# Two dense pairs of row tiles instead of three, K renumbered, and w loaded one k-slice at a time, in a Strassen-Winograd QKV projection

## The chip, the cores and the metric

The kernel runs on one core of a Trainium2 chip. The metric is device time in microseconds (us) of one execution; lower is better. Engine names are those of the profile: PE (TensorE matmul), PEld (its weight load), DVE (VectorE), ACT (ScalarE), POOL (GpSimd), SP (SyncE, which here only issues DMAs).

## The reference

One float32 matrix product, cut into three outputs:

```python
x     : (16, 512, 768) float32        # 8192 rows of K = 768
w_qkv : (768, 2304)    float32
qkv = np.matmul(x, w_qkv)
q, k, v = qkv[..., :768], qkv[..., 768:1536], qkv[..., 1536:]
return np.stack([q, k, v], axis=0).astype(np.float32)
```

x is 25.2 MB, w 7.08 MB and the output 75.5 MB.

## The kernel before, in words

**Tiling.** The 8192 rows are 32 *pairs* of 128-row tiles. The 2304 columns are two *quads* q = 0 and 1 of 1024 columns each, and a rest of 256 columns between them. K = 768 is split into KT = 6 slices of 128, which lie on the partitions; KH = 3 slices are one half. A pair and a quad together form a 2x2 by 2x2 block product (two row tiles, two halves of K, two blocks of 512 columns).

**Two ways to do a pair.** For the first NS = 3 pairs `block` does a dense product: for each quad and each of its two 512-column blocks, two row tiles times six matmuls, so 48 matmuls of 128x512 in bf16 for a pair. For pairs 3 to 31 `two` (and `last`) uses Strassen-Winograd: seven products of three matmuls per quad, so 42 for a pair. In `do(u, n)` products 1 and 2 use plain bf16 copies of x and w; products 3 to 7 use sums of blocks in f32r: of x (`s`, made by POOL in `sums_x`) and of w (`t`, made by DVE in `sum_w`; `b22` is a plain copy). Products 1, 6, 7 and 4 accumulate one after another in the same PSUM bank `u.x`, and ACT copies the bank out between them; 5 and 3 share `u.y`. I call them P1 to P7. `rem` does the 256 rest columns of a pair with 12 matmuls of 128x256.

**x.** A pair done densely is loaded by rows (`load_rows`), cast to bf16 by DVE and ACT (`cast_rows`), turned by 12 PE transposes and copied out of PSUM (`turn_rows`). A pair done with sums is loaded by `load_x` in four DMAs of 32 partitions, turned by one DVE 32x32 block transpose (`transpose`, L130), rounded to bf16 by POOL (`round_x`, L175) and summed by POOL (`sums_x`, L183 to L187).

**K numbering.** K is numbered `(p j)`: partition p holds rows 6p to 6p+5 of w. So the transposes read every sixth element, and one partition's six slices are six neighbouring rows of w.

**w.** `load_w` (L89) takes rows `"(p j) n -> p j n"` and issues one DMA for as many slices as it is given. The first block of quad 0 is loaded in six DMAs of one slice, the other three blocks in two DMAs of three slices each, and the 256 rest columns (`st_rem`) in one DMA. The blocks land in fp32 staging tiles; DVE and ACT cast them (`cast`, `cast_k`), and `sum_w` subtracts them.

**Order.** The schedule is written out by hand (`manual_schedule`): every engine runs its instructions in program order. All loads of the start are on SP's queue, in the order x0, x1, w(0,0), `st_rem`, x2, w(0,1), w(1,0), w(1,1), x3. Here w(q,c) is block c of quad q. A DMA reports on one of eight semaphores, taken in turn, and SP issues it only after the DMA eight places before it has landed. The PE order is: warm-up matmuls on zeros (`busy`, L365), transposes and the dense block (0,0) of pairs 0 and 1, their rests, pair 2's transposes and block (0,0), then blocks (0,1), (1,0), (1,1) of all three pairs, pair 2's rest, and then `two` for pair 3 onward. Stores are on SP's queue after those loads. The output tiles `o` come from a pool of five and those of the rest columns (`orem`) from a pool of two, so a tile is written again only after its store has landed.

Of the kernel before, what the change touches and what calls it, by code (L numbers as in the profile page):

```python
# [10 lines left out]
def kernel(  # L11
# [20 lines left out]
    nc = tc.nc  # L32
    P = 128
# [51 lines left out]


    def load_w(dst, j0, nj, off, cols):
        rows = w_qkv.rearrange("(p j) n -> p j n", j=KT)
        nc.sync.dma_start(dst, rows[:, j0:j0 + nj, off:off + cols])  # L89

    stage = {}

    def load_blocks(q, c, nj=KH):
        if q == 0:
            t = tq_pool.tile([P, KT, CB], fp32, name="st0", tag="tq")
            for j in range(0, KT, nj):
                load_w(t[:, j:j + nj], j, nj, Q_OFF[q] + c * CB, CB)
            stage[q, 0, c], stage[q, 1, c] = t[:, :KH, :], t[:, KH:, :]
        else:
            for h in range(2):  # L100
                t = st_pool.tile([P, KH, CB], fp32, name="st1", tag="st")
                load_w(t[:], h * KH, KH, Q_OFF[q] + c * CB, CB)
                stage[q, h, c] = t[:]

    def sum_w(q, n):
        t1, t2, t3, t4 = ts[q]
        o, in0, in1 = {
            1: (t1, stage[q, 0, 1], stage[q, 0, 0]),
            2: (t2, stage[q, 1, 1], t1),
            3: (t3, stage[q, 1, 1], stage[q, 0, 1]),  # L110
            4: (t4, stage[q, 1, 0], t2),
        }[n]
        nc.vector.tensor_tensor(o, in0, in1, op=sub)
# [5 lines left out]
    def load_x(p, other):  # L119
        xin[p] = xin_pool.tile([P, 2 * P // G, KC], fp32, name="xin")  # L120
        t = xin[p]
        rows = x_flat[p * 2 * P:(p + 1) * 2 * P, :].rearrange("(g b) k -> b g k", b=G)
        for n in range(2):
            for h in range(2):
                i = 2 * h + n
                (nc.sync, other)[h].dma_start(t[i * G:(i + 1) * G], rows[:, :, i * KC:(i + 1) * KC])

    def transpose(p):
        t = xf_pool.tile([P, KT, 2 * P], fp32, name="xf")
        nc.vector.transpose(  # L130
            t[:].rearrange("p j (g b) -> p g j b", b=G),
            xin.pop(p)[:].rearrange("p g (a j) -> p g j a", a=G),
        )
        xf[p] = t

# [2 lines left out]
    def load_rows(p):  # L138
        xin[p] = xin_pool.tile([P, 2, K], fp32, name="xin")
        rows = x_flat[p * 2 * P:(p + 1) * 2 * P, :]  # L140
        nc.sync.dma_start(xin[p][:], rows.rearrange("(r m) k -> m r k", m=P))

    def copy_halves(dst, src, two):

        nc.vector.tensor_copy(out=dst[0], in_=src[0])  # L145
        if two:
            nc.scalar.activation(dst[1], src[1], ident)  # L147
        else:
            nc.vector.tensor_copy(out=dst[1], in_=src[1])
# [3 lines left out]
    def cast_rows(p, two=True):  # L153
        src = xin.pop(p)
        xc[p] = s_pool.tile([P, 2, K], bf16, name="xc", tag="s")
        for r in range(2):
            halves = (slice(0, K // 2), slice(K // 2, K))
            copy_halves([xc[p][:, r, n] for n in halves], [src[:, r, n] for n in halves], two)

    def turn_rows(p, two=True):  # L160
        c = xc.pop(p)
        xb[p] = xb_pool.tile([P, KT, 2 * P], bf16, name="xb", tag="xb")
        for r in range(2):
            cols = c[:, r, :].rearrange("m (p j) -> m j p", j=KT)
            ps = ps_pool.tile([P, KT, P], bf16, name="ps")
            for j in range(KT):
                nc.tensor.transpose(ps[:, j, :], cols[:, j, :], eye)  # L167
            ks = (slice(0, KH), slice(KH, KT))
            copy_halves(
                [xb[p][:, n, r * P:(r + 1) * P] for n in ks], [ps[:, n, :] for n in ks], two  # L170
            )

    def round_x(p):
        xb[p] = xb_pool.tile([P, KT, 2 * P], bf16, name="xb", tag="xb")
        nc.gpsimd.tensor_copy(out=xb[p][:], in_=xf[p][:])  # L175
# [18 lines left out]
    def quad(p, q):  # L194
        u = Quad()
        u.p, u.q = p, q
        u.o = o_pool.tile([P, 2, 2 * CB], fp32, name="o", tag="o")
        u.x = u.y = u.z = None
        return u
# [67 lines left out]
    def rem(p):  # L267
        ps = ps_pool.tile([P, 2, REM], fp32, name="ps")
        for r in range(2):
            rem_row(p, r, ps[:, r, :])  # L270
        o = or_pool.tile([P, 2, REM], fp32, name="orem")
        nc.scalar.activation(o[:], ps[:], ident)  # L272
        nc.sync.dma_start(rows_of(1, p, R_OFF - H, R_OFF - H + REM), o[:])
# [67 lines left out]
        rem_stored(1)  # L341


    NS = 3
    zero = xb_pool.tile([P, CB], bf16, name="zero", tag="xb")
    nc.vector.memset(zero[:], 0.0)  # L346
    load_rows(0)
    nc.scalar.activation(tiny[:], zero[:, :1], ident)
    make_identity(nc, eye)
    load_rows(1)  # L350
    load_blocks(0, 0, 1)
    st_rem = o_pool.tile([P, KT, REM], fp32, name="str", tag="o")
    load_w(st_rem[:], 0, KT, R_OFF, REM)
    load_rows(2)
    load_blocks(0, 1)
    load_blocks(1, 0)
    load_blocks(1, 1)
    load_x(3, nc.sync)
    quads = [[quad(p, q) for p in range(NS)] for q in range(2)]

    def busy(n):

        ps = bank()
        for _ in range(n):
            nc.tensor.matmul(ps[:], zero[:, :P], zero[:], start=True, stop=True)  # L365

    def cast(q, h, c, w, eng):

        dst = w[:, h * KH:(h + 1) * KH, :]
        if eng is nc.scalar:  # L370
            eng.activation(dst, stage[q, h, c], ident)
        else:
            eng.tensor_copy(out=dst, in_=stage[q, h, c])

    def block(q, c, w, groups, cast_next):


        ps = {}
        for js, tiles in groups:
            for n in tiles:  # L380
                p, r = divmod(n, 2)
                if n not in ps:
                    ps[n] = bank()
                for j in js:
                    nc.tensor.matmul(  # L385
                        ps[n][:], xb[p][:, j, r * P:(r + 1) * P], w[:, j, :],
                        start=(j == 0), stop=(j == KT - 1), skip_group_check=True,
                    )
                if KT - 1 not in js:
                    continue  # L390
                if r == 0:
                    cast_next(p)
                u = quads[q][p]
                nc.scalar.activation(u.o[:, r, c * CB:(c + 1) * CB], ps[n][:], ident)
                if c == 1 and r == 1:
                    store_quad(u)

    def halves(tiles):
        return [(range(h * KH, (h + 1) * KH), tiles) for h in range(2)]


    singles = [((0, ), (0, 1)), ((1, ), (0, 1)), ((0, 1), (2, 3))]
    singles += [((j, ), range(4)) for j in range(2, KT)]

    act, dve = nc.scalar, nc.vector
    def cast_k(j):
        dve.tensor_copy(out=b1[0][:, j, :], in_=stage[0, j // KH, 0][:, j % KH, :])

    def cast_next(q, c, w):
        return lambda p: p < 2 and cast(q, p, c, w, act)  # L410

    def cast_k(j):
        dve.tensor_copy(out=b1[0][:, j, :], in_=stage[0, j // KH, 0][:, j % KH, :])

    nothing = lambda p: None
    busy(11)
    cast_rows(0)
    turn_rows(0)
# [7 lines left out]
    act.activation(w_rem[1][:], st_rem[:, KH:], ident)  # L426
    dve.tensor_copy(out=w_rem[0][:], in_=st_rem[:, :KH])
    bt0 = bt_pool.tile([P, KT, CB], bf16, name="bt")
    bt1 = bt_pool.tile([P, KT, CB], bf16, name="bt")

    block(0, 0, b1[0], singles, nothing)
    rem(0)
    rem(1)
    cast_rows(2, False)
    turn_rows(2, False)
    block(0, 0, b1[0], halves((4, 5)), nothing)
    for h in range(2):
        cast(0, h, 1, bt0, dve)
    for n in range(1, 5):
        sum_w(0, n)  # L440
    dve.tensor_copy(out=b22[0][:], in_=stage[0, 1, 1])
    block(0, 1, bt0, halves(range(6)), cast_next(1, 0, b1[1]))
    load_x(4, nc.sync)
    block(1, 0, b1[1], halves(range(6)), cast_next(1, 1, bt1))
    block(1, 1, bt1, halves(range(6)), nothing)
    rem(2)
    t_1 = [tq_pool.tile([P, 2, KH, CB], f32r, name=f"t_1{n}", tag="tq") for n in range(2)]
    ts[1] = [t_1[n // 2][:, n % 2] for n in range(4)]
    sum_w(1, 1)
    sum_w(1, 2)  # L450
    transpose(3)
    round_x(3)
    sums_x(3)
    sum_w(1, 3)
    sum_w(1, 4)
    dve.tensor_copy(out=b22[1][:], in_=stage[1, 1, 1])

    for p in range(NS, NP):
        def early():
            if p + 1 < NP:  # L460
                transpose(p + 1)
                round_x(p + 1)
                sums_x(p + 1)
            if p + 2 < NP:
                load_x(p + 2, nc.scalar)

        if p < NP - 1:
            two(quad(p, 0), quad(p, 1), early)
        else:
            last(quad(p, 0), quad(p, 1))  # L470
# [30 lines left out]
```

## Time and profile before

| what | value |
|---|---|
| median of 3 runs (lowest to highest) | 362.73 us (362.67 to 363.09) |
| span of the profiled execution | 361.3 us |
| the profiled execution's own time | not listed apart from its span; the median lies 1.4 us above the span |
| PE busy | 353.4 us (98%), 1765 instructions |
| DVE, ACT, POOL busy | 224.4, 182.9, 173.9 us |
| DMA | 108.08 MB, mean 299 GB/s |
| one pair of `two`, start to start | 10.74 us |
| start of pair 3 (first matmul of `two`) | 45.43 us |

How to read it: an engine's busy time is summed over the span, so it is an average over the start, the 29 like pairs and the end. The chain that ended last follows work back from the last instruction. Times within the span are us from its start. "GB/s" and "DMA share" are what the core's 16 DMA engines moved and the mean share of time in which they had packets under way; packets overlap a little, so a full share reads slightly above 1.

### The profile page before, as it was taken

The numbers are of one execution on the slowest core, as the hardware profiler recorded it, in microseconds if no ns is written. First come the engines' busy times: TensorE is split into PE (matmuls) and PEld (weight loads), VectorE is DVE, ScalarE is ACT, GpSimd is POOL, SyncE is SP. The second block draws the span as 40 slices with busy tenths as digits, with TensorE's granted clock in tenths as the row PEclk, the third lists the DMA queues.
The fourth block names the chain that finished last, engine by engine and source line by source line (L and its number), as shares of the span: only waits on it lengthen the run. The fifth ranks groups of instructions, "written<-read, shape, count | busy, mean of one in ns | idle before, by whom it ended". The sixth has DMA issues, their size and how long they took to land.

```text
span 361.3 us, 5221 instructions
## 1 busy us (share of the span) xinstructions
PE 353.4 (98%) x1765; PEld 251.0 (69%) x1797; DVE 224.4 (62%) x239; ACT 182.9 (51%) x304; POOL 173.9 (48%) x180
## 2 busy tenths in 40 slices
PE   8999999999999999999999999999999999999995
PEld 3644577777777777777777777777777777777763
DVE  3499826765566765566675565676556676556642
ACT  4547555455454545454545445455545454545452
POOL 0001861746664445664445665444665444666410
PEclk9999999999999999999999999999999999999999
DMA  7999869988898999899899999998989899999666
GB/s 298 405 388 373 286 221 359 331 289 295 278 328 301 294 273 294 276 324 315 280 280 290 281 308 309 291 289 278 292 288 321 295 300 271 297 272 339 264 261 232
DMA packets 80617, 108.08 MB, mean 299 GB/s; under 512 B 4816, under 2 KB 60368, under 8 KB 80592
## 3 DMA queue, kind: packets, MB, share of 16 engines
q1 hardware_dynamic: 65184, 96.35, 80.8%
q10 hardware_dynamic: 15408, 11.41, 9.6%
q8 instruction: 14, 0.23, 0.3%
q14 instruction: 11, 0.09, 0.1%
HBM read 32.24 MB, written 75.50 MB: 298 GB/s over the span
## 4 chain that ended last, share of the span: by engine, by line
PE 96%; ACT 1%; issue 1%; ACTq 0%; DVE 0%
PE ps L212 75%; PE ps L262 11%; PE ps L385 9%; PE ps L365 1%; PE ps L167 1%; ACT o L243 0%; ACTq L303 0%; ACT xb L147 0%; ACT orem L317 0%; DVE xb L145 0%; ACT xc L147 0%; ACTq L319 0%; DVE zero L346 0%; ACTq L317 0%
## 5 line engine op out<-in xcount | busy, mean ns | idle before, releaser
L212 PE MATMUL ps<-t,s 128*128 128x512 f32 x696 | 173.8, 398 | 0.0
L212 PEld LDWEIGHTS ps<-t,s 128*128 128x128 f32 x696 | 130.7, 188 | 29.7
L175 POOL CAST xb<-xf 128x1536 bf16<-128x1536 f32 x29 | 43.8, 1510 | 168.3 <-DVE xf L130 156.0
L240 DVE TENSOR_TENSOR o<-o,ps 128x512 f32<-128x512 f32 x58 | 39.9, 688 | 91.2 <-ACT o L239 91.2
L130 DVE STREAM_TRANSPOSE xf<-xin 128x1536 f32<-128x1536 f32 x29 | 85.5, 2950 | 3.7 <-DMA out_dram<-orem 2.1
L212 PE MATMUL ps<-b,xb 128*128 128x512 bf16 x320 | 82.4, 380 | 1.5
L239 ACT ACTIVATE o<-ps 128x512 f32<-128x512 f32 x58 | 34.8, 600 | 44.2 <-PE ps L212 44.2
L212 PEld LDWEIGHTS <-xb 128*128 128x128 bf16 x348 | 31.7, 98 | 35.6 <-issue 7.3
L233 ACT ACTIVATE o<-ps 128x512 f32<-128x512 f32 x58 | 34.9, 601 | 42.1 <-PE ps L212 39.4
L246 DVE TENSOR_TENSOR o<-o,ps 128x512 f32<-128x512 f32 x58 | 39.9, 688 | 21.3 <-PE ps L212 20.2
L212 PE MATMUL ps<-b,s 128*128 128x512 f32 x174 | 48.7, 389 | 0.0
L262 PE MATMUL ps<-w_rem,xb 128*128 128x256 bf16 x384 | 47.2, 273 | 0.0
L243 ACT ACTIVATE o<-ps 128x512 f32<-128x512 f32 x58 | 34.7, 599 | 24.1 <-PE ps L212 21.3
L226 ACT ACTIVATE o<-ps 128x512 f32<-128x512 f32 x58 | 34.7, 598 | 23.8 <-DVE o L246 20.6
L262 PEld LDWEIGHTS <-xb 128*128 128x128 bf16 x384 | 37.4, 98 | 11.2 <-issue 0.5
L230 DVE TENSOR_TENSOR o<-o,ps 128x512 f32<-128x512 f32 x58 | 36.5, 673 | 5.4 <-PE ps L212 4.1
L212 PEld LDWEIGHTS ps<-b,s 128*128 128x128 f32 x174 | 32.7, 188 | 6.8
L184 POOL TENSOR_TENSOR s<-s,xf 128x384 fp32r<-128x384 f32 x29 | 30.0, 1035 | 2.3
L183 POOL TENSOR_TENSOR s<-xf 128x384 fp32r<-128x384 f32 x29 | 30.9, 1064 | 0.0
L185 POOL TENSOR_TENSOR s<-xf 128x384 fp32r<-128x384 f32 x29 | 29.5, 1017 | 0.0
L187 POOL TENSOR_TENSOR s<-xf,s 128x384 fp32r<-128x384 f32 x29 | 29.5, 1016 | 0.0
L272 ACT ACTIVATE orem<-ps 128x512 f32<-128x512 f32 x31 | 18.5, 598 | 20.7 <-PE ps L262 19.5
(36 smaller groups left out, 129.4 us busy)
## 6 DMA issues: line engine op xcount, KB each, us to landing
out_dram<-o SPq DMA_DIRECT2D x62, 768.0 KB, 4.8
out_dram<-o SPq DMA_DIRECT2D x65, 256.0 KB, 4.1
xin<-in_x_dram SPq DMA_DIRECT2D x62, 192.0 KB, 6.9
xin<-in_x_dram ACTq DMA_DIRECT2D x54, 192.0 KB, 4.4
out_dram<-orem SPq DMA_DIRECT2D x31, 256.0 KB, 5.7
st<-in_w_qkv_dram SPq DMA_DIRECT2D x6, 768.0 KB, 13.1
xin<-in_x_dram SPq DMA_DIRECT2D x3, 768.0 KB, 5.7
st<-in_w_qkv_dram SPq DMA_DIRECT2D x6, 256.0 KB, 6.1
```

Source lines behind the costliest of these rows:

```text
L130: nc.vector.transpose(t[:].rearrange("p j (g b) -> p g j b", b=G), xin.pop(p)[:].rearrange("p g (a j) -> p g j a", a=G),)
L175: nc.gpsimd.tensor_copy(out=xb[p][:], in_=xf[p][:])
L212: nc.tensor.matmul(ps[:], lhs[j], rhs[j], start=(start and j == 0), stop=(j == KH - 1), skip_group_check=True,)
L226: nc.scalar.activation(c11, u.x[:], ident)
L230: nc.vector.tensor_tensor(c11, c11, u.z[:], op=add)
L233: nc.scalar.activation(c12, u.x[:], ident)
L239: nc.scalar.activation(c22, u.x[:], ident)
L240: nc.vector.tensor_tensor(c22, c22, u.y[:], op=add)
L243: nc.scalar.activation(c21, u.x[:], ident)
L246: nc.vector.tensor_tensor(c12, c12, u.y[:], op=add)
L262: nc.tensor.matmul(ps, xb[p][:, j, r * P:(r + 1) * P], w_rem[j // KH][:, j % KH, :], start=(j == 0), stop=(j == KT - 1), skip_group_check= ...
L385: nc.tensor.matmul(ps[n][:], xb[p][:, j, r * P:(r + 1) * P], w[:, j, :], start=(j == 0), stop=(j == KT - 1), skip_group_check=True,)
```

## The change

- **w.** K is numbered `(i j a)` with i of 4, j of 6 slices and a of 32: partition p = 32 i + a of slice j is row 192 i + 32 j + a of w. A slice's partitions are then four separate runs of 32 neighbouring rows, and `load_w` issues one DMA per slice, everywhere. `load_blocks(0, 0, 1)` becomes `load_blocks(0, 0)`. The start has 30 w DMAs where it had 13.
- **x.** `transpose` reads 32 neighbouring elements at a time; `cast_rows` writes its bf16 copy already ordered by slice, so that the PE transposes read neighbouring elements.
- **Pairs.** Only pairs 0 and 1 (ND = 2) are dense. Pair 2 is loaded with `load_x` and done with sums, quad by quad, by the new function `alone`: P1, P2, P6, P5, P7, P3, and its P4 later.
- **Order.** Loads on SP: x0, x1, w(0,0), `st_rem`, w(0,1), x2, w(1,0), w(1,1), x3. PE: block (0,0) and the rests of pairs 0 and 1, their block (0,1), then pair 2's quad 0 with its rest, block (1,0), P4 of quad 0, block (1,1), pair 2's quad 1, and `two` for pair 3, in which quad 1's P4 follows both P1s. The rest of pair 2 is the third user of the two `orem` tiles and now stands between P2 and P6 of pair 2's quad 0; ACT's copy of it waits for the first `orem` store, and that store follows all the loads on SP's queue.

```diff
     def load_w(dst, j0, nj, off, cols):
-        rows = w_qkv.rearrange("(p j) n -> p j n", j=KT)
-        nc.sync.dma_start(dst, rows[:, j0:j0 + nj, off:off + cols])
+        rows = w_qkv.rearrange("(i j a) n -> i a j n", i=4, a=G)
+        for j in range(nj):
+            nc.sync.dma_start(dst[:, j], rows[:, :, j0 + j, off:off + cols])
...
-            xin.pop(p)[:].rearrange("p g (a j) -> p g j a", a=G),
+            xin.pop(p)[:].rearrange("p g (j a) -> p g j a", a=G),
...
-            halves = (slice(0, K // 2), slice(K // 2, K))
-            copy_halves([xc[p][:, r, n] for n in halves], [src[:, r, n] for n in halves], two)
+            turned = xc[p][:, r].rearrange("m (j i a) -> m i j a", i=4, a=G)
+            rows = src[:, r].rearrange("m (i j a) -> m i j a", i=4, a=G)
+            halves = (slice(0, 2), slice(2, 4))
+            copy_halves([turned[:, n] for n in halves], [rows[:, n] for n in halves], two)
...
-            cols = c[:, r, :].rearrange("m (p j) -> m j p", j=KT)
+            cols = c[:, r, :].rearrange("m (j p) -> m j p", j=KT)
...
-    NS = 3
+    ND = 2
...
-    load_blocks(0, 0, 1)
+    load_blocks(0, 0)
     st_rem = o_pool.tile([P, KT, REM], fp32, name="str", tag="o")
     load_w(st_rem[:], 0, KT, R_OFF, REM)
-    load_rows(2)
     load_blocks(0, 1)
+    load_x(2, nc.sync)
     load_blocks(1, 0)
     load_blocks(1, 1)
     load_x(3, nc.sync)
...
+    def alone(u, between):
+        c22 = u.o[:, 1, CB:]
+        do(u, 1)
+        do(u, 2)
+        between()
+        do(u, 6)
+        do(u, 5)
+        act.activation(c22, u.y[:], ident)
+        product(u, 7, u.x, False)
+        dve.tensor_tensor(c22, c22, u.x[:], op=add)
+        do(u, 3)
+
+    def ahead(p):
+        transpose(p)
+        round_x(p)
+        sums_x(p)
...
-    block(0, 0, b1[0], singles, nothing)
+    block(0, 0, b1[0], singles)
     rem(0)
     rem(1)
-    cast_rows(2, False)
-    turn_rows(2, False)
-    block(0, 0, b1[0], halves((4, 5)), nothing)
-    for h in range(2):
-        cast(0, h, 1, bt0, dve)
-    for n in range(1, 5):
-        sum_w(0, n)
+    cast(0, 0, 1, bt0, dve)
+    cast(0, 1, 1, bt0, act)
+    block(0, 1, bt0, halves(range(4)))
+    sum_w(0, 1)
+    sum_w(0, 2)
+    ahead(2)
+    sum_w(0, 3)
+    sum_w(0, 4)
     dve.tensor_copy(out=b22[0][:], in_=stage[0, 1, 1])
-    block(0, 1, bt0, halves(range(6)), cast_next(1, 0, b1[1]))
+    u = quad(2, 0)
+    def between():
+        cast(1, 0, 0, b1[1], act)
+        rem(2)
+    alone(u, between)
+    cast(1, 1, 0, b1[1], act)
     load_x(4, nc.sync)
-    block(1, 0, b1[1], halves(range(6)), cast_next(1, 1, bt1))
-    block(1, 1, bt1, halves(range(6)), nothing)
-    rem(2)
...
+    for h in range(2):
+        cast(1, h, 1, bt1, act)
+    block(1, 0, b1[1], halves(range(4)))
+    do(u, 4)
+    store_quad(u)
     sum_w(1, 1)
     sum_w(1, 2)
-    transpose(3)
-    round_x(3)
-    sums_x(3)
+    ahead(3)
     sum_w(1, 3)
     sum_w(1, 4)
     dve.tensor_copy(out=b22[1][:], in_=stage[1, 1, 1])
-    for p in range(NS, NP):
+    block(1, 1, bt1, halves(range(4)))
+    u = quad(2, 1)
+    alone(u, lambda: None)
+    for p in range(ND + 1, NP):
         def early():
+            if p == ND + 1:
+                do(u, 4)
+                store_quad(u)
```

More of the change, by code (lines that the diff above doesn't have):

```diff
@@ L358 @@
     load_x(3, nc.sync)
-    quads = [[quad(p, q) for p in range(NS)] for q in range(2)]
     def busy(n):
@@ L365, in busy @@
             nc.tensor.matmul(ps[:], zero[:, :P], zero[:], start=True, stop=True)
+    act, dve = nc.scalar, nc.vector
     def cast(q, h, c, w, eng):
         dst = w[:, h * KH:(h + 1) * KH, :]
-        if eng is nc.scalar:
+        if eng is act:
             eng.activation(dst, stage[q, h, c], ident)
@@ L373, in cast, with cast_k, block @@
             eng.tensor_copy(out=dst, in_=stage[q, h, c])
-    def block(q, c, w, groups, cast_next):
+    def cast_k(j):
+        dve.tensor_copy(out=b1[0][:, j, :], in_=stage[0, j // KH, 0][:, j % KH, :])
+    quads = {}
+    def block(q, c, w, groups):
         ps = {}
@@ L390, in block @@
                     continue
[L391 to L394, printed above, removed]
+                if (p, q) not in quads:
+                    quads[p, q] = quad(p, q)
+                u = quads[p, q]
+                act.activation(u.o[:, r, c * CB:(c + 1) * CB], ps[n][:], ident)
                 if c == 1 and r == 1:
@@ L399, in halves @@
         return [(range(h * KH, (h + 1) * KH), tiles) for h in range(2)]
+    def alone(u, between):
[13 more added lines that the diff above has]
+        sums_x(p)
     singles = [((0, ), (0, 1)), ((1, ), (0, 1)), ((0, 1), (2, 3))]
     singles += [((j, ), range(4)) for j in range(2, KT)]
[L405 to L415, printed above, removed]
     busy(11)
@@ L428 @@
     bt0 = bt_pool.tile([P, KT, CB], bf16, name="bt")
-    bt1 = bt_pool.tile([P, KT, CB], bf16, name="bt")
-    block(0, 0, b1[0], singles, nothing)
+    block(0, 0, b1[0], singles)
     rem(0)
     rem(1)
-    cast_rows(2, False)
-    turn_rows(2, False)
-    block(0, 0, b1[0], halves((4, 5)), nothing)
-    for h in range(2):
-        cast(0, h, 1, bt0, dve)
-    for n in range(1, 5):
-        sum_w(0, n)
-    dve.tensor_copy(out=b22[0][:], in_=stage[0, 1, 1])
-    block(0, 1, bt0, halves(range(6)), cast_next(1, 0, b1[1]))
+    cast(0, 0, 1, bt0, dve)
[6 more added lines that the diff above has]
+    sum_w(0, 4)
+    dve.tensor_copy(out=b22[0][:], in_=stage[0, 1, 1])
+    u = quad(2, 0)
[4 more added lines that the diff above has]
+    cast(1, 1, 0, b1[1], act)
     load_x(4, nc.sync)
-    block(1, 0, b1[1], halves(range(6)), cast_next(1, 1, bt1))
-    block(1, 1, bt1, halves(range(6)), nothing)
-    rem(2)
     t_1 = [tq_pool.tile([P, 2, KH, CB], f32r, name=f"t_1{n}", tag="tq") for n in range(2)]
     ts[1] = [t_1[n // 2][:, n % 2] for n in range(4)]
+    bt1 = bt_pool.tile([P, KT, CB], bf16, name="bt")
+    for h in range(2):
[3 more added lines that the diff above has]
+    store_quad(u)
     sum_w(1, 1)
     sum_w(1, 2)
-    transpose(3)
-    round_x(3)
-    sums_x(3)
+    ahead(3)
     sum_w(1, 3)
@@ L456 @@
     dve.tensor_copy(out=b22[1][:], in_=stage[1, 1, 1])
-    for p in range(NS, NP):
+    block(1, 1, bt1, halves(range(4)))
+    u = quad(2, 1)
+    alone(u, lambda: None)
+    for p in range(ND + 1, NP):
         def early():
+            if p == ND + 1:
+                do(u, 4)
+                store_quad(u)
             if p + 1 < NP:
-                transpose(p + 1)
-                round_x(p + 1)
-                sums_x(p + 1)
+                ahead(p + 1)
             if p + 2 < NP:
```

## The prediction

> **What bounds the kernel now.** I read the page first: busy times, the chain that ended last, the groups. PE is busy nearly all the span and carries the chain, so a change is worth what it does to PE's order of work: fewer matmuls, or new waits in front of them.
>
> ```profile
> PE 353.4 (98%) x1765; PEld 251.0 (69%) x1797; DVE 224.4 (62%) x239; ACT 182.9 (51%) x304; POOL 173.9 (48%) x180
> ...
> PE 96%; ACT 1%; issue 1%; ACTq 0%; DVE 0%
> ```
>
> Then the chain in order of time, which gives the price of a step at the start:
>
> ```profile
> 1.19 4.88 PE ps L365 x11
> ...
> 14.64 2.62 PE ps L262 x24
> 17.26 0.35 PE ps L167 x6
> ...
> 18.49 10.74 PE ps L385 x49
> ...
> 44.12 1.31 PE ps L262 x12
> 45.43 1.30 PE ps L212 x6
> 46.73 1.31 PE ps L262 x12
> ```
>
> Columns are start, us, engine and line. From 18.05 to 44.12 us stand the 120 dense matmuls that follow pair 2's transposes: 26.07/120 = 0.2172 us each. A pair in `two` takes 10.74 us from rest to rest, 1.31 of it the rest, so its 30 f32r matmuls take (10.74 - 1.31 - 12 x 0.2172)/30 = 0.2275 each. The first eleven matmuls after idleness took 4.88/11 = 0.444 each: a cold run of PE costs 11 x (0.444 - 0.217) = 2.5 us.
>
> Last I read the start in windows, and what waited for the w loads:
>
> ```profile
> 4.00:26.00 22.00, 21.25 (x128) 11.79 (x129) 14.77 (x29) 10.86 (x19) 0.00 (x0) 1.00 1.05 405
> ```
> ```profile
> 12.91 0.84 ACT L426 ACTIVATE w_rem<-str 128x768 bf16<-128x768 f32 x1 [2.52 <-DMA str<-in_w_qkv_dram]
> ...
> 21.84 1.49 ACT L371 ACTIVATE b<-st 128x1536 bf16<-128x1536 f32 x1 [0.39 <-DMA st<-in_w_qkv_dram]
> ```
>
> The last three numbers of the window are granted clock, DMA share and GB/s: while w streams in, all 16 engines are full (1.05) at 405 GB/s, or 25.3 GB/s for one. Casts wait for the landing by 2.52 and 0.39 us: the start already runs just behind the loads, and a slower w reaches PE at once.
>
> **The change, part by part.** I take the start of pair 3's first matmuls (45.43 us) as the mark, since everything after it is unchanged, and ask where it goes.
>
> *PE work.* From the end of the two rests (17.26) the new order needs 72 dense matmuls (15.64 us), 42 of pair 2 (9.43) and its rest (1.31): 26.4 us, so the mark could stand at 43.6, which is 1.8 us earlier. Of this 1.0 is six matmuls fewer, 0.8 pair 2's transposes and their wait.
>
> *The w loads.* Bytes are the same. What changes is the cut: a slice's source now has an outermost count of 4 (four runs of 32 rows), its destination 128. Every load in the profile has outermost counts of 32, 128 or 768 on both sides, all multiples of 16, and those fill 16 engines. No row shows one with fewer. The bounds are nothing (the work is dealt out row by row, 405 GB/s as before) and a quarter (outermost pieces are dealt to the engines, four engines take part, 4 x 25.3 = 101 GB/s). I take the quarter, since the rows agree with dealing out outermost pieces and four pieces cannot feed sixteen engines. [...]
>
> In KB per engine on the four, in queue order: x0 and x1 98, w(0,0) 393, `st_rem` 197, w(0,1) 393, x2 49, w(1,0) 393, w(1,1) 393, x3 49, the first `orem` store 16. Sum 1982 KB, at 25.3 GB/s 78.4 us (w alone 70). The stream starts at about 2.3 (the window from 2 to 4 us has share 0.85) and landings follow 0.9 after the data: `st_rem` is complete after 3.93 MB, 9.7 us, so at 12.0, and its casts start at 12.91. SP keeps eight DMAs under way, so the queue does not run dry.
>
> *Where PE then stands.* w(0,1) is in at about 46, x2 at 48; the transpose (2.95), rounding (1.46) and sums of POOL, DVE's sums and pair 2's P1, P2 and rest are done by 58, with PE waiting most of the time. Then ACT stops: its copy of pair 2's rest needs an `orem` tile whose store is queued behind all loads, so it lands at 2.3 + 78.4 + 0.9 = 81.6. Queued behind this copy on ACT are the copy after P6 (which P7 and P3 need, then block (1,0)) and three casts of w(1,.).
>
> *From there.* ACT's two copies of 0.60 each with their hops: P7 starts at 82.9. PE then does 54 bf16 matmuls (P1, P2 and two blocks; 11.7 us) and 21 f32r (4.8): 16.5. Add one cold run, 2.5, since PE has idled for some 25 us. In `alone`, P6, P7 and P3 each wait for an ACT copy of 0.60 that one product of 0.68 covers: 0.3 together. The mark comes to 102.2. P4 of quad 1 is left inside pair 3, 0.7. Delay: 102.9 - 45.4 = 57.5 us. DVE's second chain is covered: t sums 3.5, transpose 2.95, t sums 3.5, copy up to 1.75 from 86.1 end at 97.8, and the product that wants the last copy starts near 101. So are casts of 1.49 on ACT, which end at 88.4 while block (1,0) runs to 91.
>
> *The rest, with one answer.* The x casts with 32-element runs (0.36 on DVE, 0.52 on ACT before) could cost up to twice as much or gain a little; both lie ahead of w slices that now land 2.6 us apart. The issue of 17 more DMAs (0.37 to 0.65 each, 11 us at most) is hidden in a stream of 78. From pair 4 on, the DVE transpose (2.94, or faster) is on an engine that is 62% busy and behind PE: nothing. Stores held back until 82 are some 2.6 MB, 6.5 us at 405 GB/s, before tiles are wanted again at 102.
>
> *Sum.* Span 361.3 + 57.5 = 418.8; what lies around the span is 362.73 - 361.3 = 1.4 if the profiled execution is like the median one: 420.2, say 420.
>
> **Rivals.**
>
> *A, full rate: faster.* If the w DMAs use all 16 engines, loads land as before. w(0,1)'s first half lands near 15, so DVE goes cast 0.95, two t sums 1.75, then the transpose of pair 2 from 19.3. With 2.95 it ends at 22.2 and POOL's rounding at 23.7; PE wants P1 at 22.5, so it waits 1.2, plus the 0.3 in `alone`: gain 0.3. If contiguous blocks bring the transpose near DVE's other op on as many elements (1.75, L113), the wait goes: gain 1.5. So 361.2 to 362.4, middle 361.8. For it: nothing in the profile forbids it. Against it: four outermost pieces. [...]
>
> *B, a quarter for each DMA, but a different quarter each time.* Eight under way then cover all engines and only first landings suffer: a slice takes 2.6 us instead of 0.65, the first cast is 1.7 later than in A: 363.5. Nothing in the profile tells which engines a short DMA takes.
>
> *C, a quarter, but the held store doesn't decide.* If the store passed the loads, w(1,1) would: landed at 79.0, x3 at 81.0, transpose to 84.0, t sums to 87.5, copy to 88.4, the last product of `alone` then. Mark 89.1, delay 44.4: 407. It speaks against this that on the same four engines the store stands in queue order.
>
> **How the numbers follow.** Forecast 0.74, C 0.09, A 0.13, B 0.04. The forecast's own spread: without the cold run 417.7; if one engine's rate is 25.3/1.05 (the share read as plain time) 3.9 more, 424; a second cold run 2.5 more, 427. C reaches down to 405 without its cold part. The range 405 to 427 covers forecast and C, about 0.8. A measurement of this kernel can tell about 0.2% (0.7 us) from no change. Faster by more is most of A, 0.08; within it 0.05; slower 0.87.
>
> **What would show it.** Right: GB/s falling to about 100 and DMA share to about a quarter between 6 and 80 us; w slices landing 2.6 us apart; ACT's rest copy of pair 2 released near 82 by a store; pair 3 near 102; 10.74 per pair afterward. A: share 1.0 to 27 us, as before, and pair 3 near 45. C: the last long PE wait ends on DVE's copy of w near 88. The forecast fails most simply if the DMA share at 10 us is still 1.0.

## The result, and the profile after

The changed kernel takes 423.85 us (median of 4 runs, 422.92 to 424.88) against 362.70 before: ratio 1.1687, 95% interval 1.1667 to 1.1708. The profiled execution took 424.23 us, of which 422.4 are its span. The forecast was 420 us (405 to 427).

The page of the changed kernel, the lines that answer to those shown of before:

```profile
PE 366.8 (87%) x1747; PEld 255.1 (60%) x1779; DVE 199.5 (47%) x237; ACT 184.6 (44%) x305; POOL 183.0 (43%) x186
...
GB/s 190 102 98 132 111 102 115 262 206 269 228 274 306 284 296 295 293 293 291 305 282 292 297 294 295 294 284 307 280 308 289 295 290 293 289 281 305 311 219 278
...
PE 78%; SPq 7%; issue 7%; DMA 4%; POOL 2%; ACT 1%; ACTq 0%
```

PE's share fell from 98% to 87%, and a fifth of the chain is now SP's queue, DMA and waits. The GB/s row has 40 slices of 10.6 us: the first seven hold the start at 98 to 190, where the kernel before moved 405 from 4 to 26 us; from the twelfth on the row lies near 290, as it does in the kernel before.

Windows of the changed kernel (columns as before: PE, PEld, DVE, ACT, POOL, granted clock, DMA share, GB/s):

```profile
10.00:20.00 10.00, 5.21 (x15) 1.81 (x16) 2.01 (x6) 0.87 (x2) 0.00 (x0) 0.83 0.26 102
30.00:40.00 10.00, 5.38 (x23) 3.18 (x23) 1.76 (x2) 3.98 (x7) 0.00 (x0) 0.50 0.36 123
40.00:50.00 10.00, 4.95 (x12) 1.77 (x12) 2.62 (x2) 1.48 (x1) 0.00 (x0) 0.67 0.38 121
60.00:70.00 10.00, 0.83 (x4) 0.36 (x2) 0.00 (x0) 0.00 (x0) 1.49 (x3) 0.73 0.26 102
70.00:78.00 8.00, 0.00 (x0) 0.00 (x0) 0.00 (x0) 0.00 (x0) 0.00 (x0) 0.50 0.49 150
82.00:84.00 2.00, 0.00 (x0) 0.00 (x0) 0.00 (x0) 0.00 (x0) 0.00 (x0) 0.50 1.03 384
```

While w alone streams, the DMA share is 0.26, as much as four engines of sixteen, at 102 GB/s: 25.5 GB/s for one of four, where each of the sixteen had 25.3 before. From 30 to 50 us, while pair 2's x is loaded too, the share rises to 0.36 and 0.38. In steps of 1 us it is 0.42 to 0.76 from 38 to 44 us, although w(0,1), ahead of x2 on the queue, is in only near 47.8: DMAs of the one queue do run side by side. From 70 to 84 us every compute engine stands still. The order of time shows the pace and what ends the standstill:

```profile
12.10 0.43 DVE L380 CAST b<-st 128x512 bf16<-128x512 f32 x1 [2.13 <-DMA st<-in_w_qkv_dram]
...
14.67 0.43 DVE L380 CAST b<-st 128x512 bf16<-128x512 f32 x1 [1.61 <-DMA st<-in_w_qkv_dram]
...
17.23 0.43 DVE L380 CAST b<-st 128x512 bf16<-128x512 f32 x1 [2.13 <-DMA st<-in_w_qkv_dram]
...
38.23 0.96 DVE L377 CAST bt<-st 128x1536 bf16<-128x1536 f32 x1 [11.23 <-DMA st<-in_w_qkv_dram]
...
47.80 1.48 ACT L375 ACTIVATE bt<-st 128x1536 bf16<-128x1536 f32 x1 [11.11 <-DMA st<-in_w_qkv_dram]
...
57.59 1.48 ACT L375 ACTIVATE b<-st 128x1536 bf16<-128x1536 f32 x1 [1.10 <-DMA st<-in_w_qkv_dram]
...
85.03 0.60 ACT L275 ACTIVATE orem<-ps 128x512 f32<-128x512 f32 x1 [25.95 <-DMA out_dram<-orem]
```

A slice lands every 2.57 us. At 85.03 the first `orem` store has landed and ACT copies pair 2's rest, for which it stood 25.95 us. The chain from there, to pair 3's first products and its rest:

```profile
86.21 2.90 PE ps L215 x6
...
95.71 0.69 PE ps L215 x3
...
106.39 1.94 PE ps L215 x8
108.33 1.33 PE ps L265 x12
```

Pair 3's rest starts at 108.33 where it started at 46.73: 61.6 us later. From that rest to the end of the span it is 314.1 us, before 314.6.

### The profile page after: what moved, and what is told of

Read it like the earlier page. It is cut to its first block, busy times and chain, and to the rows that moved or that the text cites. A ratio compares the mean times of both kernels' runs of the same rounds, so it can differ in the third digit from the quotient of the medians.

```text
span 422.4 us, 5232 instructions
## 1 busy us (share of the span) xinstructions
PE 366.8 (87%) x1747; PEld 255.1 (60%) x1779; DVE 199.5 (47%) x237; ACT 184.6 (44%) x305; POOL 183.0 (43%) x186
## 4 chain that ended last, share of the span: by engine, by line
PE 78%; SPq 7%; issue 7%; DMA 4%; POOL 2%; ACT 1%; ACTq 0%
PE ps L215 66%; PE ps L265 9%; SPq L90 7%; DMA st<-in_w_qkv_dram 4%; PE ps L394 3%; POOL xb L178 1%; POOL s L186 1%; POOL s L187 0%; ACT bt L375 0%; ACT o L246 0%; ACTq L306 0%; POOL s L188 0%; POOL s L190 0%; SPq L142 0%; ACT orem L320 0%
## 5 line engine op out<-in xcount | busy, mean ns | idle before, releaser
L215 PE MATMUL ps<-t,s 128*128 128x512 f32 x720 | 181.8, 400 | 26.8 <-issue 25.4
L215 PEld LDWEIGHTS ps<-t,s 128*128 128x128 f32 x720 | 135.3, 188 | 59.1 <-issue 25.8
L178 POOL CAST xb<-xf 128x1536 bf16<-128x1536 f32 x30 | 46.7, 1557 | 219.5 <-DVE xf L131 135.1
L243 DVE TENSOR_TENSOR o<-o,ps 128x512 f32<-128x512 f32 x58 | 39.9, 688 | 94.7 <-ACT o L242 94.7
L215 PEld LDWEIGHTS <-xb 128*128 128x128 bf16 x360 | 32.7, 98 | 38.4 <-issue 7.9
L236 ACT ACTIVATE o<-ps 128x512 f32<-128x512 f32 x60 | 35.9, 599 | 43.6 <-PE ps L215 40.9
L233 DVE TENSOR_TENSOR o<-o,ps 128x512 f32<-128x512 f32 x60 | 40.2, 688 | 31.4 <-ACT orem L275 22.5
L265 PE MATMUL ps<-w_rem,xb 128*128 128x256 bf16 x384 | 49.9, 282 | 5.9 <-ACT w_rem L442 3.5
L242 ACT ACTIVATE o<-ps 128x512 f32<-128x512 f32 x58 | 34.7, 598 | 44.3 <-PE ps L215 44.3
L131 DVE STREAM_TRANSPOSE xf<-xin 128x1536 f32<-128x1536 f32 x30 | 53.2, 1772 | 0.7 <-DMA xin<-in_x_dram 0.7
L249 DVE TENSOR_TENSOR o<-o,ps 128x512 f32<-128x512 f32 x60 | 41.3, 688 | 21.9 <-PE ps L215 20.8
L215 PE MATMUL ps<-b,s 128*128 128x512 f32 x180 | 51.1, 393 | 0.0
L265 PEld LDWEIGHTS <-xb 128*128 128x128 bf16 x384 | 38.3, 101 | 19.2 <-issue 4.6
L229 ACT ACTIVATE o<-ps 128x512 f32<-128x512 f32 x60 | 35.8, 597 | 26.4 <-DVE o L249 21.4
L246 ACT ACTIVATE o<-ps 128x512 f32<-128x512 f32 x60 | 35.9, 598 | 24.3 <-PE ps L215 21.3
L186 POOL TENSOR_TENSOR s<-xf 128x384 fp32r<-128x384 f32 x30 | 33.4, 1114 | 0.0
L394 PEld LDWEIGHTS <-xb 128*128 128x128 bf16 x96 | 11.2, 119 | 33.6 <-issue 24.7
```

Source lines behind the costliest of these rows:

```text
L131: nc.vector.transpose(t[:].rearrange("p j (g b) -> p g j b", b=G), xin.pop(p)[:].rearrange("p g (j a) -> p g j a", a=G),)
L186: g.tensor_tensor(s[:, 1], a21, a22, op=add)
L215: nc.tensor.matmul(ps[:], lhs[j], rhs[j], start=(start and j == 0), stop=(j == KH - 1), skip_group_check=True,)
L229: nc.scalar.activation(c11, u.x[:], ident)
L233: nc.vector.tensor_tensor(c11, c11, u.z[:], op=add)
L236: nc.scalar.activation(c12, u.x[:], ident)
```

## The experiments

Each is compared with the kernel before, run beside it on the same chip (362.58 to 362.85 us). "Mark" is the start of pair 3's rest within the span: 46.73 before, 108.33 in the changed kernel.

### Many small DMAs, outermost count still 128

```diff
-        nc.sync.dma_start(dst, rows[:, j0:j0 + nj, off:off + cols])
+        for j in range(nj):
+            nc.sync.dma_start(dst[:, j], rows[:, j0 + j, off:off + cols])
```

> The kernel before, with one edit: w is loaded by one DMA per slice everywhere (30 DMAs instead of 13), K still numbered so that the source's outermost count is 128. My theory (the four outermost pieces confine a load to four of sixteen engines): nothing happens, 362.2 to 363.5 us, and the loads still run at about 400 GB/s up to 26 us. Rival (many small DMAs, each waiting for the one eight places before, are what slows w): w at well under 400 GB/s and a time above 370, up to 420.

Measured 362.69 us, ratio 1.0004 (0.9994 to 1.0014). The window over the loads:

```profile
4.00:26.00 22.00, 21.04 (x131) 11.49 (x132) 14.37 (x28) 11.19 (x21) 0.00 (x0) 1.00 1.05 401
```

Share 1.05 and 401 GB/s, as before (1.05, 405). The number of DMAs, their size and the waits between them cost nothing here: it is not "one DMA per slice" that slows w.

### Outermost count 2 instead of 4

```diff
-            nc.sync.dma_start(dst[:, j], rows[:, :, j0 + j, off:off + cols])
+            for i in (0, 2):
+                nc.sync.dma_start(dst[i * G:(i + 2) * G, j], rows[i:i + 2, :, j0 + j, off:off + cols])
```

> The changed kernel, with one edit: each slice of w is loaded by two DMAs of 64 partitions, whose source has an outermost count of 2. My theory: a load uses as many engines as it has outermost pieces, and always the same ones, so two: w at about 51 GB/s, its part of the stream from 69 to about 139 us, a time of 424 + 70 = 494 us (485 to 500), DMA share about an eighth between 10 and 140 us. Rival (the short runs of 32 rows are slow in themselves, whatever the count): the same rate as the changed kernel, about 102 GB/s, and 424 us give or take 5. Rival (a different set of engines for each DMA): 102 GB/s or more too.

Measured 493.11 us in one run. Windows and the order of time:

```profile
10.00:20.00 10.00, 2.92 (x7) 0.94 (x7) 1.38 (x4) 0.87 (x2) 0.00 (x0) 0.54 0.13 51
...
110.00:130.00 20.00, 0.00 (x0) 0.00 (x0) 0.00 (x0) 0.00 (x0) 0.00 (x0) 0.50 0.13 51
```
```profile
12.48 0.43 DVE L381 CAST b<-st 128x512 bf16<-128x512 f32 x1 [5.05 <-DMA st<-in_w_qkv_dram]
17.61 0.43 DVE L381 CAST b<-st 128x512 bf16<-128x512 f32 x1 [4.70 <-DMA st<-in_w_qkv_dram]
```

Half the count, half the share (0.13, as much as two of sixteen), half the rate, and 5.13 us per slice. The rival of slow 32-row runs would have left the rate alone. DMAs run side by side (from 38 to 44 us above), and in the changed kernel the last slice of w(0,1), issued at 32.55 us, landed 15.15 us later while one slice followed another at 2.57, so several were under way. Yet with w alone the share stays at two engines' worth here, and at four there: each seems to take the same ones, and rival B is out. The three counts run here gave 401 to 405 GB/s (128), 102 (4) and 51 (2). Which engines they were by number, no run here shows.

### K numbering and w loads alone, three dense pairs

The kernel before with the new `load_w`, `transpose`, `cast_rows` and `turn_rows`, and nothing of the new order.

> The kernel before with the other half of the change alone: K renumbered and w loaded in four runs per slice, but three dense pairs in the old order. My theory: the quarter rate alone costs most of it. The rest of pair 2 comes at the end here, so no store holds ACT; w(1,1) lands near 81, its cast ends near 83, PE does the second half of the last block cold, pair 2's rest and pair 3's start near 90: 362.7 + 44 = 407 us (402 to 412). Rival (the order of pairs is what costs): below 375.

Measured 409.24 us (one run), mark 92.54. So the new numbering with its loads costs 46.7 us in the old order, where the whole change costs 61; the rival (below 375) is out. In this run x2 is loaded by rows, ahead of w(0,1), and the casts that wait for three slices each stand at 48.56, 56.24 and 63.93 us: 7.7 apart.

### Pair 2's rest copied elsewhere

```diff
...
-        rem(2)
+        rem(2, stage[0, 0, 1][:, 0, :].rearrange("p (r n) -> p r n", r=2))
```

`rem`, in lines left out here, now writes into the tile that it is given. Here that is a staging tile of w, no longer read by then.

> The changed kernel, with one edit: ACT's copy of pair 2's rest goes into the first slice of a w staging tile that is no longer read, so that it no longer waits for the first orem store. The loads of w stay cut into four runs. My theory has two parts: w arrives at a quarter of the rate, and the store queued behind the loads holds ACT until it lands (85.0 us in the changed kernel). If both hold, w(1,1) decides instead: it lands near 83, x3 near 84, transpose 1.8, three DVE ops on w to about 93; pair 3's rest starts near 95 to 97 instead of 108.3, so 410 to 413 us. Rival: the hold costs nothing, since w(1,1) and its chain of casts and sums set the mark in any case; then 422 to 425.

Measured 416.32 us, ratio 1.1479 (1.1456 to 1.1502), mark 101.09: 7.5 us less than the changed kernel, so the hold is real. It missed the expectation by 3 to 6 us, and the trace says why:

```profile
91.86 2.25 DVE L114 TENSOR_TENSOR t<-st,st 128x1536 fp32r<-128x1536 f32 x1 [5.36 <-DMA out_dram<-st]
```

The staging tile's memory is used again by a later t sum (a difference of two blocks of w), so now DVE waits 5.36 us for the store that reads it. My edit moved the hold and shortened it; so I take 7.5 us as a lower bound of its price.

### The new order alone, at full rate

The changed kernel with the old `load_w`, `transpose`, `cast_rows` and `turn_rows`; then the same with pair 2's rest copied elsewhere.

> The changed kernel without its K numbering: w, x and the transposes as in the kernel before (outermost count 128, 405 GB/s), two dense pairs and pair 2 with sums as in the change. My theory: the loads are back to 27 us, and what is left is the new order. Its work would put the mark at 43.6 instead of 45.4, but DVE's old transpose (2.95 us) makes P1 wait 1.2 us, and ACT's copy of pair 2's rest still waits for a store behind all loads, landing near 29, which holds P7 by 2.6 us; with 0.6 in the lone quad the mark is near 48: 365 us (363.5 to 367). Rival (the new order is sound, only w's cut was bad): 361 to 362.3.

> As the run before it, and ACT's copy of pair 2's rest goes into a w staging tile, so that it waits for no store. My theory: the 2.6 us of the hold go, the wait for the transpose stays: 362.7 us (361.5 to 364), about 2.6 below the run before it. Rival (the hold costs nothing at full rate): the same time as the run before it.

Measured 369.84 us, ratio 1.0194 (1.0180 to 1.0208), mark 53.89; and 367.39, ratio 1.0145 (1.0121 to 1.0168), mark 51.60. The hold costs 2.5 us, where 2.6 were expected, but both runs stand 4.7 to 4.8 us above what I expected. The run with the hold:

```profile
21.56 2.90 DVE L130 STREAM_TRANSPOSE xf<-xin 128x1536 f32<-128x1536 f32 x1 [2.40 <-DMA xin<-in_x_dram]
...
24.52 2.90 POOL L175 CAST xb<-xf 128x1536 bf16<-128x1536 f32 x1 [23.22 <-DVE xf L130]
...
27.48 2.74 PE L212 MATMUL ps<-b,xb 128*128 128x512 bf16 x6 [5.58 <-POOL xb L175]
...
33.31 0.60 ACT L272 ACTIVATE orem<-ps 128x512 f32<-128x512 f32 x1 [2.37 <-DMA out_dram<-orem]
```

PE waits 5.58 us for pair 2's rounding, where I had 1.2. x2 starts its transpose at 21.56 instead of 19.3, and POOL's rounding takes 2.90 beside DVE's t sums instead of 1.46. P1 and P2 then run cold: six matmuls in 2.74 us, where six took 1.30 before. In the run without the hold they took 2.27, and the granted clock from 26 to 28 us reads 0.71, where it was 1.00 before. So the new order of pairs, with fewer matmuls, is slower than the old one also at full rate, by 7.0 us with the hold and 4.5 without; the rival (361 to 362.3) is out. The new numbering with its loads costs 46.7 us by itself and the order 7.0, together they cost 61.2: some 7.5 us arise only where the two meet.

### 32 partitions to a DMA: sixteen engines, new numbering

```diff
-        for j in range(nj):
-            nc.sync.dma_start(dst[:, j], rows[:, :, j0 + j, off:off + cols])
+        for i in (0, 2, 1, 3):
+            nc.sync.dma_start(dst[i * G:(i + 1) * G], rows[i, :, j0:j0 + nj, off:off + cols])
```

> The changed kernel with w loaded by four DMAs of 32 partitions and three (or six) slices each: the source's outermost count is 32, a multiple of 16, K numbering and order as changed. My theory: the loads use all engines again, and the time falls from 424 to 365 if 32 partitions take the full 405 GB/s (the hold of ACT by the store, about 4 us, stays, as the faster transpose brings P1 earlier and the hold ends at the same time); only x3 shows 32-partition loads in the profile of before, in a window of 258 GB/s, and at that rate the loads end near 40 and the time is up to 377. Rival (runs of 32 rows are slow whatever the outermost count): above 400.

> As the run before it, and the rest of pair 2 copied into a w staging tile. My theory: with full-rate loads, contiguous transposes and no hold the change shows what it could bring: 361.2 to 361.8 us, less than before; at 258 GB/s the loads set the mark near 50 and it is 367.

Measured 382.38 us, ratio 1.0536 (1.0521 to 1.0551), and 375.11, ratio 1.0338 (1.0324 to 1.0352). The first of them in windows:

```profile
10.00:20.00 10.00, 8.91 (x44) 4.73 (x45) 3.29 (x9) 3.97 (x8) 0.00 (x0) 0.83 1.09 248
```

All sixteen engines are busy (1.09), and the time falls by 41 us without a change of numbering: the runs of 32 rows do not hold w at 102 GB/s, the count of 4 did. But the loads move 248 GB/s, not 405, and both times lie above the slow end of what I expected (377 and 367), by 5 and 8 us that I did not take apart. The hold costs 7.3 us here (382.38 - 375.11), where I had about 4.

### x2 first

The new order at full rate with pair 2's rest copied elsewhere, and with x2 loaded ahead of w(0,1), its transpose first on DVE, and w(0,1)'s first half cast by ACT in three pieces; then also the lone quad as P1, P2, P5, P6, P3, P7.

> Full-rate loads in the old K numbering, two dense pairs, pair 2's rest into a staging tile, and now x2 loaded ahead of w(0,1), its transpose first on DVE, and the first half of w(0,1) cast by ACT slice by slice. My theory: in the run with the rest elsewhere PE waited 4.0 us for pair 2's rounding on POOL (2.90 us long beside DVE's sums) and ran cold after it; with x2 landed at 15 the rounding ends near 21 and the sums for P6 near 25, before PE asks at 22.6 and 25.2, so the wait and the cold run go: 367.4 - 5 = 362.4 us (361.3 to 363.5). Rival (the rounding is not what set the pace, the loads of w(0,1) are): 365 to 367, as PE then waits at the first block of w(0,1).

> As the run before it, with the lone quad in the order P1, P2, P5, P6, P3, P7, so that two products instead of one stand between most copies and the product that needs them. My theory: the waits of P6, P7 and P3 for ACT's copies (0.58, 0.42 and 0.17 us in the changed kernel's second lone quad) mostly go, 0.5 to 1 us less than the run before it: about 361.7. Rival: the same time, since P3 now comes earlier and waits for the last sum of x.

Measured 366.46 us, ratio 1.0106 (1.0093 to 1.0120), and 368.32, ratio 1.0146 (1.0127 to 1.0165). Neither came out as expected; the first lies in its rival's range (365 to 367). In it, w(0,1) landed later and the sums grew on both engines:

```profile
18.14 1.67 ACT L447 ACTIVATE bt<-st 128x512 bf16<-128x512 f32 x3 [1.80 <-DMA st<-in_w_qkv_dram]
18.82 2.75 PE L392 MATMUL ps<-bt,xb 128*128 128x512 bf16 x12 [2.16 <-ACT bt L447]
...
23.82 2.55 DVE L113 TENSOR_TENSOR t<-st 128x1536 fp32r<-128x1536 f32 x1
...
24.84 2.39 POOL L184 TENSOR_TENSOR s<-s,xf 128x384 fp32r<-128x384 f32 x1
...
31.91 0.96 PE L212 MATMUL ps<-b,s 128*128 128x512 f32 x3 [1.18 <-POOL s L187]
```

DVE's sum takes 2.55 instead of 1.75 and POOL's 2.39 instead of 1.0 while both run, and PE waits for w (2.16) and at the end for POOL's last sum (1.18). The second run has two times at 366.7, the same as the first run, as its rival said, and three near 368.4. In those three the mean granted clock is 0.991 against 1.000, so some part of them was cold; what started that, and whether it makes up the 1.7 us, I did not settle. No version here beats the kernel before.

## Why the prediction was right

**The quarter rate: right, and shown.** It was a choice between two bounds that no row could decide. Outermost counts of 128, 4 and 2, with a slice of w or half of one to a DMA, gave 401 to 405, 102 and 51 GB/s: sixteen, four and two engines' worth. The new numbering with its loads made 409 us by itself.

**The stream: right in kind, one term too small.** `st_rem` was cast from 30.53 us, worked out 30.4; the store landed at 85.03, worked out 81.6. The term that was too small is x2, which I charged by its bytes, 1.9 us. Three slices take 7.7 us where nothing lies among them; the two triples around x2's four DMAs took 47.80 - 38.23 = 9.6 and 57.59 - 47.80 = 9.8. So x2 cost 4.0 us, twice its bytes, which is 2.1 of the 3.4 us missing. The other 1.3 I put down to x3, loaded in the same way, but no run prices it apart. Whether the 768-byte pieces of x do that was not tried either.

**The hold of ACT: right.** ACT waited 25.95 us for the store, and taking that wait off gave 7.5 us in spite of a new one on DVE. No run of the new order at a quarter of the rate stands without any hold, so rival C's 407 us was not tested.

**From there to pair 3: 0.9 short.** P7 started at 86.21 and pair 3's products at 106.39, 20.2 us instead of 19.3. The cold run was right in kind and 0.4 short: the granted clock reads 0.50 from 70 to 84 us, and P7 and P3, six matmuls, then take 2.90 us. Up to the end of block (1,0), at 95.71, PE took 9.50 us for what is 6.58 at full rate, so 2.9 us were lost to the cold instead of 2.5. The waits for ACT's copies in the lone quad were taken at 0.3; its last twelve matmuls took 3.34 us, which are 2.73 by their rate, and with two short gaps the waits come to some 0.8.

**The sum.** 61.6 us of delay instead of 57.5, a span of 422.4 instead of 418.8; the stretch after pair 3's rest was taken as unchanged and is 0.5 shorter.

**Rival A was priced wrong,** though it did not come about. At full rate and with the old transpose the new order is 7.0 us slower, where A's sum has it 0.3 faster; its 1.5 for a quick transpose was not tested, since no run had that and 405 GB/s together. A's sum left out the hold, which the forecast had (2.5 us), took x2's landing 2.3 us too early, and used POOL's rounding from a row where it ran by itself (1.46), while the same trace of the kernel before has one of 2.80 beside DVE's sums:

```profile
34.68 2.80 POOL L175 CAST xb<-xf 128x1536 bf16<-128x1536 f32 x1 [33.37 <-DVE xf L130]
...
36.05 3.03 DVE L113 TENSOR_TENSOR t<-st,t 128x1536 fp32r<-128x1536 f32 x1
...
45.54 1.46 POOL L175 CAST xb<-xf 128x1536 bf16<-128x1536 f32 x1 [1.55 <-PE ps L262]
```

Nor did it have the cold P1 and P2 that follow PE's wait, some 1.4 us.

## What to carry to other kernels

Look at the outermost count of the source of every DMA, not only at the bytes of its runs: renumbering an axis for one engine's sake made four row blocks out of 128 rows, and the DMA share fell from 1.05 to 0.26 and the rate from 405 to 102 GB/s. When the start of a kernel runs just behind its loads, follow one step further to what is queued behind them: here a store that frees an output tile held ACT, and with it PE, at least 7.5 us longer than w would have. And before taking matmuls away from PE, price the sums that replace them beside each other: POOL's rounding took 2.90 us beside DVE's t sums here, and 1.46 alone.

## What the runs showed of the hardware that I had not expected

- **A busy share is not a rate.** Loads of w in DMAs of 32 partitions each, with DMAs to other partitions following in the same queue, read a share of 1.09 and moved 248 GB/s; in DMAs of 128 partitions it was 1.05 and 405. What holds the first at 248, no run here shows.
- **DVE and POOL took longer side by side.** POOL's rounding took 1.46 us alone and 2.80 to 2.90 beside t sums, its first sum 1.0 and 2.5; DVE's t sum took 1.75 alone and up to 3.03 beside POOL (2.50 and 2.55 with x2 first). Which of them lost differed: in the kernel before, the t sum under way when the rounding began (34.42 us) took 1.73 and the next one 3.03; in the run at full rate with pair 2's rest elsewhere, a later rounding took 5.37 while the t sums beside it took 1.70 and 1.74. What decides that was not tried.
- **The block transpose gained from neighbours.** Reading 32 neighbouring elements instead of every sixth, its time fell by two fifths:

```profile
L131 DVE STREAM_TRANSPOSE xf<-xin 128x1536 f32<-128x1536 f32 x30 | 53.2, 1772 | 0.7 <-DMA xin<-in_x_dram 0.7
```

Before it was 2950 ns; for a quick one rival A had 1.75 us, the time of DVE's t sum. Thirty of them free DVE of some 35 us, but from pair 3's rest to the end the kernel gained only 0.5 us (314.1 against 314.6): there DVE is not what PE waits for.
